# Two 256-column matmuls into one accumulator in place of one 512-column matmul and a fold

## The chip, the cores and the metric

The kernel runs on one core of one Trainium2 chip. The metric is the device time of one execution in microseconds (us); 2125.77 us is the median of 3 runs of the kernel before (2125.0 to 2126.07).

The core's engines run beside each other: PE (TensorE) does matmuls, and its weight loads are listed apart as PEld; DVE (VectorE) and ACT (ScalarE) do elementwise work and are the only two that read the matmuls' results out of PSUM here; POOL (GpSimd) does a little arithmetic; SP issues the DMAs. PSUM has eight banks, each of 512 fp32 columns on 128 partitions.

## The reference

A trunk of two residual layers on 256 tokens of width 2048: sparse attention with an MLP, then a gated short convolution with an MLP. Attention, norms and rotary embedding are left out here; what the change touches are the two kinds of product below, whose weights are read once each.

```python
def _short_conv_mixer(h, w_in, conv_w, w_out):
    b_gate, c_gate, u = jnp.split(h @ w_in, 3, axis=-1)       # w_in 2048 x 6144
    z = c_gate * u
    zp = jnp.pad(z, ((0, 0), (CONV_WIDTH - 1, 0), (0, 0)))
    y = sum(zp[:, j:j + S] * conv_w[j] for j in range(CONV_WIDTH))
    return (b_gate * y) @ w_out

def _sqrelu_mlp(h, w1, w2):
    a = jax.nn.relu(h @ w1)                                    # w1 2048 x 8192
    return (a * a) @ w2                                        # w2 8192 x 2048
...
for i in range(DEPTH):                                         # DEPTH = 2
    x = x + mixer(_rmsnorm(x, g))                              # 0: attention, 1: short conv
    x = x + _sqrelu_mlp(_rmsnorm(x, mlp_norm_g[i]), mlp_w1[i], mlp_w2[i])
```

## The kernel before

All large products are made in fp32 accuracy from float32r parts: each operand is the sum of a high part and a low part, and of the four products three are kept (high by high, high by low, low by high). The weights arrive by DMA as `raw` tiles; `split` (lines 202 and 203) makes from each the high part `wh` on ACT and the low part `wl` on DVE, four pieces ahead of PE. The tokens' operand tiles (`xp` from a norm, `hq` from a product) hold for one k-tile of 128 rows 256 columns of high parts and then 256 columns of low parts.

The work is a list of units. A unit is one accumulation over K into a set of PSUM banks, cut into pieces; the main loop at the end of the program takes one piece at a time: its matmuls (`matmuls`, line 210), at the unit's last piece the unit's `end`, one step of every generator of side work, and then the splits of pieces further on. The order on each engine is the order in which this loop emits instructions. There are two kinds of unit:

- Wide units (lines 229 to 231): the tokens' tile is the stationary operand, the weights stream past in 512 columns (384 and 336 in the first unit), three matmuls for each k-tile and bank.
- Tall units (lines 224 and 225): the weights are stationary, 128 output columns at a time, and the tokens stream past. They are used where the result is wanted with features on partitions: the first product of both MLPs (32 units) and the input product of the convolution (12 units). A tall unit makes 512 output columns in four blocks, each with a bank of its own (`W4`, line 849), from 16 k-tiles in 8 pieces of two. For a block and a k-tile, `wh` is matched with all 512 token columns, so that the bank's left half gathers high by high and its right half high by low; then `wl` is matched with the 256 high columns and adds into the left half. That is 44 x 4 x 16 = 2,816 pairs of matmuls.

At the end of a tall unit the halves of each bank are added: `fold` (line 760) copies the right half to SBUF on ACT (line 763) and adds the left half to it on DVE (line 764); `fold4` does so for the four banks. For an MLP, `h_gen` then squares the positive part (line 781, DVE) and `put_pair` (lines 756 and 757) splits the result into high and low for the next wide unit. In an MLP two tall units are followed by two wide ones that use their results; the first four k-tiles of the wide unit come from the first of the two tall ones, the next four from the second.

Of the kernel before, what the change touches and what calls it, by code (L numbers as in the profile page):

```python
# [18 lines left out]
P = 128  # L19
# [20 lines left out]

# 500000 ** -(j / 16), j = 0..15, then 500000 ** -(j / 8), j = 0..7, in float32
_F16 = [
# [11 lines left out]
class Unit:  # L54
    """One accumulation group over K, in ticks of kk k-tiles, on n columns of a weight.

    wide: out[token, column], banks of the given column widths for each of two token tiles.
    tall: out[column, (token by x high part, token by x low part)], a bank for 128 columns.
    """

# [8 lines left out]
def trunk(ctx: ExitStack, tc: tile.TileContext, x, positions, attn_norm_g, attn_w_in, attn_q_norm_g,  # L69
# [21 lines left out]

# [1 line left out]
    live = []  # L93
# [38 lines left out]

# [1 line left out]
    ident = sb.tile([P, P], F32, name="ident")  # L134
# [22 lines left out]

# [1 line left out]
    units = []  # L159
# [50 lines left out]
    def matmuls(p):  # L210
        u, i, _ = pieces[p]
        n, K = u.n, u.kk * u.ticks
        if i == 0:
            u.banks = [[bank() for _ in u.widths] for _ in range(1 if u.tall else 2)]
        hi, lo = piece_tiles.pop(p)
        for t, row in enumerate(u.banks):
            c = 0
            for o, w in zip(row, u.widths):
                for j in range(u.kk):
                    k = i * u.kk + j  # L220
                    wh, wl = (v[:, j * n + c : j * n + c + w] for v in (hi, lo))
                    xk = u.lhs(k)
                    if u.tall:
                        nc.tensor.matmul(o, wh, xk, start=(k == 0), stop=False)  # L224
                        nc.tensor.matmul(o[:, 0:256], wl, xk[:, 0:256], start=False, stop=(k == K - 1))  # L225
                    else:
                        ah = xk[:, t * P : (t + 1) * P]
                        al = xk[:, 256 + t * P : 256 + (t + 1) * P]
                        nc.tensor.matmul(o[:, :w], ah, wh, start=(k == 0), stop=False)  # L229
                        nc.tensor.matmul(o[:, :w], al, wh, start=False, stop=False)  # L230
                        nc.tensor.matmul(o[:, :w], ah, wl, start=False, stop=(k == K - 1))  # L231
                c += w

# [1 line left out]
    def rsqrt(v, n):  # L235
        """v**-0.5 for a [P, n] tile, by a bit guess and three Newton steps."""
        y, t = small(n), small(n)
        yi = y.bitcast(I32)
        nc.vector.tensor_scalar(yi, v.bitcast(I32), 1, None, op0=ALU.logical_shift_right)
        nc.vector.tensor_scalar(yi, yi, -1, 0x5F3759DF, op0=ALU.mult, op1=ALU.add)  # L240
        for _ in range(3):
            nc.gpsimd.tensor_tensor(t, y, y, ALU.mult)  # L242
            nc.gpsimd.tensor_tensor(t, t, v, ALU.mult)
            nc.gpsimd.tensor_scalar(t, t, -0.5, 1.5, op0=ALU.mult, op1=ALU.add)
            nc.gpsimd.tensor_tensor(y, y, t, ALU.mult)
        return y

# [1 line left out]
    def norm_gen(st, half):  # L249
        """Operand tiles of x*g for k-tiles of one half, and its part of the squares' sum."""  # L250
        if st["key"] != "attn":
# [61 lines left out]
    def norm_rows(key, power):  # L313
        """The token scale (or its square) of a norm along the free axis, [P, 256]."""
        st = norms[key]
        yield from wait((key, "rs"))
        yield from pause(3)
        rows = tmp()[:, 0:256]
        dg = tmp()
        for t in range(2):  # L320
            nc.vector.tensor_scalar(
                dg[:, t * P : (t + 1) * P], ident, st[power][:, t : t + 1], None, op0=ALU.mult
            )
        nc.vector.memset(dg[:, 256:384], 1.0)
        ps = yield from tp_get()
        yield
        for t in range(2):
            nc.tensor.matmul(
                ps[:, t * P : (t + 1) * P], dg[:, 256:384], dg[:, t * P : (t + 1) * P],
                start=True, stop=True,  # L330
            )
        yield
        nc.scalar.activation(rows, ps[:, 0:256], AF.Copy)
        tp_put()
        st[power + "rows"] = rows
        done.add((key, power + "rows"))
# [30 lines left out]

# [1 line left out]
    def add_to_x(nh, then=None, store=False, norm=None):  # L369
        def end(banks):  # L370
            for t in range(2):
                for b in range(2):
                    # the last bank of all leaves in two parts
                    w = 256 if store and nh and t and b else 512
                    for o in range(0, 512, w):
                        c = nh * 1024 + b * 512 + o
                        sl, ps = xs[t][:, c : c + w], banks[t][b][:, o : o + w]
                        if norm is None:
                            nc.vector.tensor_tensor(sl, ps, sl, ALU.add)
                        else:  # L380
                            rs_of(norm, t)
                            nc.vector.scalar_tensor_tensor(  # L382
                                sl, ps, norms[norm]["rs2"][:, t : t + 1], sl, op0=ALU.mult, op1=ALU.add
                            )
                        if store:
                            nc.sync.dma_start(out[0][t * P : (t + 1) * P, c : c + w], sl)
# [10 lines left out]

# [1 line left out]
    rope = sb.tile([P, 2, 4, RH + RI], F32, name="rope")  # L399
    NF = RH + RI  # L400

    def rope_tables():
        """rope[:, t, 0:4] = cos, cos, -sin, sin of position * frequency."""
        yield from pause(10)
# [24 lines left out]
    def rotate(v, t, heads, half, off):  # L429
        """Partial rotary on v [P, heads, dim] in place: its first 2*half dims."""  # L430
        c = rope[:, t, 0:2, off : off + half].unsqueeze(1).to_broadcast([P, heads, 2, half])
# [123 lines left out]
    def head_scale(sq, n, mul):  # L555
        """(mean of squares + eps)**-0.5 * mul from a list of squared [P, n*HD] tiles."""
        v = small(n * len(sq))
# [79 lines left out]
    def q_gen(n, qs, sqs):  # L637
# [16 lines left out]
        yield from wait("bias", "kT")  # L654
        # scores; a chunk is (token tile, heads, keys)
        chunks = [(0, (0, 1, 2, 3)), (1, (0, 1)), (1, (2, 3))]
# [77 lines left out]

# [1 line left out]
    Q = {}  # L736
# [12 lines left out]
    def put_pair(key, q, i, val):  # L749
        """Split [P, (2, 256)] fp32 into k-tiles 2i, 2i+1 of a quad."""  # L750
        if i == 0:
# [7 lines left out]

    def fold(dst, ps):  # L760
        """dst [P, 256] = the sum of a tall bank's two halves."""
        h = sbt([P, 256], "half", 4)
        nc.scalar.activation(h, ps[:, 256:512], AF.Copy)  # L763
        nc.vector.tensor_tensor(dst, ps[:, 0:256], h, ALU.add)  # L764

    def fold4(banks):
        r = [tmp(), tmp()]
        for c in range(4):
            fold(r[c // 2][:, c % 2 * 256 : (c % 2 + 1) * 256], banks[0][c])
        return r  # L770

# [1 line left out]
    def m1_end(key, q):  # L773
        def end(banks):
            live.append(h_gen(key, q, fold4(banks)))

        return end

    def h_gen(key, q, r):
        for i in range(2):  # L780
            nc.vector.scalar_tensor_tensor(r[i], r[i], 0.0, r[i], op0=ALU.max, op1=ALU.mult)  # L781
            put_pair(key, q, i, r[i])
            yield

# [1 line left out]
    C = {}  # L786

    def c_end(q):
        def end(banks):
            C["c", q] = fold4(banks)  # L790

        return end

    def u_end(q):
        def end(banks):
            live.append(y_gen(q, fold4(banks)))

        return end

    def b_end(q):  # L800
        def end(banks):
            live.append(by_gen(q, fold4(banks)))

# [42 lines left out]

# [1 line left out]
    W2 = [512, 512]  # L848
# [37 lines left out]

# [1 line left out]

# [16 lines left out]

    # transposes of no use but to have the tensor engine's clock up when x arrives
    ps = bank()
# [57 lines left out]
```

## Time and profile before

| | before |
|---|---|
| median of 3 runs | 2125.77 us |
| span of the profiled execution, first to last instruction | 2122.9 us |
| PE busy | 2112.0 us, 99% of the span |
| PEld busy | 1788.8 us, 84% |
| DVE busy | 1286.4 us, 61% |
| ACT busy | 977.2 us, 46% |
| POOL busy | 114.8 us, 5% |
| DMA | 392.66 MB, mean 185 GB/s |
| matmuls, weight loads | 10,714 and 10,714 |

The profiled execution is listed with its span alone; the medians are 2.9 us above it. Busy times of different engines overlap and don't add up to the span. A matmul is listed with a duration of its own that overlaps the next one's, since they are pipelined; what a matmul costs in a dense row of them is the distance from its start to the start of the next, called a step below.

### The profile page before, as it was taken

Reading aid. Unit: us, or ns where it says so; the run is one execution under the profiler, and the core shown is the slowest. Engines: PE = TensorE matmul, PEld = TensorE weight load, DVE = VectorE, ACT = ScalarE, POOL = GpSimd, SP = SyncE. Lnnn points to the kernel's source line nnn. Section 1 sums busy time; section 2 is a strip of 40 time slices with the busy share of each in tenths; the row PEclk is TensorE's granted clock in tenths of the full one; section 3 lists DMA queues with packets and bytes.
Section 4 is the critical chain, followed back from the end, with each engine's and each line's share of the span. In section 5 each row is a group of like instructions: output and inputs, shape, how many; then the busy total and the mean of one; then the engine's idle time right before and its main releaser. Section 6 shows DMA issues by size and latency. Waiting matters only on the chain.

```text
span 2122.9 us, 26675 instructions
## 1 busy us (share of the span) xinstructions
PE 2112.0 (99%) x10714; PEld 1788.8 (84%) x10714; DVE 1286.4 (61%) x1553; ACT 977.2 (46%) x1271; POOL 114.8 (5%) x220
## 2 busy tenths in 40 slices
PE   9999999999999999999999999999999999999999
PEld 8878778888888888888888888888888888888887
DVE  5587656655656556556666566556565565655654
ACT  5456545443444434444555454454444344443443
POOL 0333100000000000000011110001000000000000
PEclk9999999999999999999999999999999999999999
DMA  8544455556555565565555555556655566555653
GB/s 274 173 141 163 139 177 170 188 184 206 183 189 189 180 205 181 189 198 179 183 194 179 198 179 190 196 169 202 195 184 191 181 198 193 183 190 188 199 186 111
DMA packets 152268, 392.66 MB, mean 185 GB/s; under 512 B 6368, under 2 KB 7088, under 8 KB 152144
## 3 DMA queue, kind: packets, MB, share of 16 engines
q1 hardware_dynamic: 151888, 390.75, 56.6%
q8 instruction: 84, 1.38, 0.2%
q0 software_dynamic: 224, 0.19, 0.1%
q14 instruction: 40, 0.33, 0.0%
q10 hardware_dynamic: 32, 0.01, 0.0%
HBM read 388.83 MB, written 2.10 MB: 184 GB/s over the span
## 4 chain that ended last, share of the span: by engine, by line
PE 98%; POOL 1%; DMA 1%; DVE 0%; ACT 0%; issue 0%; SPq 0%; DVEq 0%; ACTq 0%
PE ps L224 30%; PE ps L230 16%; PE ps L231 16%; PE ps L229 16%; PE ps L225 16%; DMA raw<-in_attn_w_in 1%; PE ps L278 1%; PE ps L661 0%; PE ps L507 0%; PE ps L719 0%; PE ps L706 0%; POOL tmp L440 0%; POOL rot L436 0%; PE ps L646 0%; POOL tmp L439 0%; ACT wh L202 0%
## 5 line engine op out<-in xcount | busy, mean ns | idle before, releaser
L203 DVE TENSOR_TENSOR wl<-raw,wh 128x1024 fp32r<-128x1024 f32 (+2 forms) x738 | 890.1, 1225 | 551.7 <-ACT wh L202 551.1
L202 ACT ACTIVATE wh<-raw 128x1024 fp32r<-128x1024 f32 (+2 forms) x738 | 765.9, 1055 | 722.8 <-PE ps L230 390.2
L224 PE MATMUL ps<-xp,wh 128*128 128x512 f32 x2816 | 978.0, 392 | 0.0
L225 PE MATMUL ps<-xp,wl 128*128 128x256 f32 x2816 | 786.9, 279 | 0.0
L224 PEld LDWEIGHTS ps<-xp,wh 128*128 128x128 f32 x2816 | 529.8, 188 | 114.6
L225 PEld LDWEIGHTS ps<-xp,wl 128*128 128x128 f32 x2816 | 531.6, 189 | 0.8
L231 PE MATMUL ps<-wl,hq 128*128 128x512 f32 x1280 | 505.0, 395 | 0.0
L229 PE MATMUL ps<-wh,hq 128*128 128x512 f32 x1280 | 505.0, 395 | 0.0
L230 PE MATMUL ps<-wh,hq 128*128 128x512 f32 x1280 | 505.0, 395 | 0.0
L229 PEld LDWEIGHTS ps<-wh,hq 128*128 128x128 f32 x1280 | 240.9, 188 | 55.7 <-issue 0.5
L230 PEld LDWEIGHTS ps<-wh,hq 128*128 128x128 f32 x1280 | 240.3, 188 | 56.3 <-issue 0.5
L231 PEld LDWEIGHTS ps<-wl,hq 128*128 128x128 f32 x1280 | 240.7, 188 | 54.8
L764 DVE TENSOR_TENSOR tmp<-ps,half 128x256 f32<-128x256 f32 x176 | 74.7, 424 | 110.0 <-ACT half L763 110.0
L763 ACT ACTIVATE half<-ps 128x256 f32<-128x256 f32 x176 | 67.6, 384 | 152.3 <-PE ps L225 152.3
L382 DVE SCALAR_TENSOR_TENSOR x<-ps,rs_mlp,x 128x512 f32<-128x512 f32 x129 | 90.8, 746 | 53.0 <-PE ps L231 53.0
L229 PE MATMUL ps<-wh,xp 128*128 128x512 f32 (+2 forms) x288 | 114.2, 397 | 2.2 <-ACT wh L202 2.0
L230 PE MATMUL ps<-wh,xp 128*128 128x512 f32 (+2 forms) x288 | 108.0, 375 | 0.9 <-DVE xp L263 0.9
L231 PE MATMUL ps<-wl,xp 128*128 128x512 f32 (+2 forms) x288 | 108.1, 375 | 0.4 <-DVE wl L203 0.4
L756 ACT ACTIVATE hq<-tmp 128x512 fp32r<-128x512 f32 x72 | 45.5, 632 | 105.4 <-DVE tmp L781 93.0
L757 DVE TENSOR_TENSOR hq<-tmp,hq 128x512 fp32r<-128x512 f32 x72 | 51.1, 710 | 50.3 <-ACT hq L756 50.3
L242 POOL TENSOR_TENSOR small<-small 128x8 f32<-128x8 f32 (+1 forms) x27 | 14.0, 517 | 1011.3 <-DVE small L240 1009.7
L229 PEld LDWEIGHTS ps<-wh,xp 128*128 128x128 f32 x288 | 54.6, 190 | 12.5 <-ACT wh L202 2.4
(131 smaller groups left out, 661.9 us busy)
## 6 DMA issues: line engine op xcount, KB each, us to landing
raw<-in_mlp_w SPq DMA_DIRECT2D x256, 1024.0 KB, 5.4
raw<-in_conv_w_in SPq DMA_DIRECT2D x48, 1024.0 KB, 5.2
raw<-in_attn_w_in SPq DMA_DIRECT2D x24, 1024.0 KB, 5.3
raw<-in_attn_w_out SPq DMA_DIRECT2D x16, 1024.0 KB, 5.4
raw<-in_conv_w_out SPq DMA_DIRECT2D x16, 1024.0 KB, 5.4
raw<-in_attn_w_in SPq DMA_DIRECT2D x5, 1104.0 KB, 8.2
raw<-in_attn_w_in SPq DMA_DIRECT2D x5, 552.0 KB, 8.7
out_y<-x SPq DMA_DIRECT2D x7, 256.0 KB, 2.9
```

The lines of the kernel that those rows point to most:

```text
L202: nc.scalar.activation(hi[:, a], src[:, a], AF.Copy)
L203: nc.vector.tensor_tensor(lo[:, a], src[:, a], hi[:, a].bitcast(F32), ALU.subtract)
L224: nc.tensor.matmul(o, wh, xk, start=(k == 0), stop=False)
L225: nc.tensor.matmul(o[:, 0:256], wl, xk[:, 0:256], start=False, stop=(k == K - 1))
L229: nc.tensor.matmul(o[:, :w], ah, wh, start=(k == 0), stop=False)
L230: nc.tensor.matmul(o[:, :w], al, wh, start=False, stop=False)
L231: nc.tensor.matmul(o[:, :w], ah, wl, start=False, stop=(k == K - 1))
L382: nc.vector.scalar_tensor_tensor(sl, ps, norms[norm]["rs2"][:, t : t + 1], sl, op0=ALU.mult, op1=ALU.add)
L756: nc.scalar.activation(hi, val, AF.Copy)
L757: nc.vector.tensor_tensor(lo, val, hi.bitcast(F32), ALU.subtract)
L763: nc.scalar.activation(h, ps[:, 256:512], AF.Copy)
L764: nc.vector.tensor_tensor(dst, ps[:, 0:256], h, ALU.add)
```

## The change

In a tall unit the 512-column matmul is cut in two of 256 columns with the same `wh`: high columns and low columns of the tokens both add into the same 256 columns of PSUM, and `wl` adds there too. A block needs 256 columns, so two blocks share a bank, and a unit takes two banks where it took four. The bank's first matmul carries the start flag, for the left block alone. At the end there is nothing to fold: for the convolution `copied` moves each bank to SBUF on ACT; for the MLP ACT takes the positive part out of PSUM, and DVE multiplies it by the positive part read from PSUM. The wide units stand as they were (their three matmuls are only indented anew), and comments are gone from the file.

```diff
@@ matmuls
-            u.banks = [[bank() for _ in u.widths] for _ in range(1 if u.tall else 2)]
+            u.banks = [[bank() for _ in u.widths[::2]]] if u.tall else [[bank() for _ in u.widths] for _ in range(2)]
         hi, lo = piece_tiles.pop(p)
+        if u.tall:
+            for c in range(len(u.widths)):
+                o = u.banks[0][c // 2][:, c % 2 * 256 : c % 2 * 256 + 256]
+                for j in range(u.kk):
+                    k = i * u.kk + j
+                    wh, wl = (v[:, j * n + c * P : j * n + (c + 1) * P] for v in (hi, lo))
+                    xk = u.lhs(k)
+
+                    for w, x, first, last in (
+                        (wh, xk[:, 0:256], k == 0 and c % 2 == 0, False),
+                        (wh, xk[:, 256:512], False, False),
+                        (wl, xk[:, 0:256], False, k == K - 1),
+                    ):
+                        nc.tensor.matmul(o, w, x, start=first, stop=last, skip_group_check=True)
+            return
...
-                    if u.tall:
-                        nc.tensor.matmul(o, wh, xk, start=(k == 0), stop=False)
-                        nc.tensor.matmul(o[:, 0:256], wl, xk[:, 0:256], start=False, stop=(k == K - 1))
...
-    def fold(dst, ps):
-        """dst [P, 256] = the sum of a tall bank's two halves."""
-        h = sbt([P, 256], "half", 4)
-        nc.scalar.activation(h, ps[:, 256:512], AF.Copy)
-        nc.vector.tensor_tensor(dst, ps[:, 0:256], h, ALU.add)
-
-    def fold4(banks):
+    def copied(banks):
         r = [tmp(), tmp()]
-        for c in range(4):
-            fold(r[c // 2][:, c % 2 * 256 : (c % 2 + 1) * 256], banks[0][c])
+        for i in range(2):
+            nc.scalar.activation(r[i], banks[0][i], AF.Copy)
         return r
...
     def m1_end(key, q):
         def end(banks):
-            live.append(h_gen(key, q, fold4(banks)))
+            r = [tmp(), tmp()]
+            for i in range(2):
+                nc.scalar.activation(r[i], banks[0][i], AF.Relu)
+                nc.vector.scalar_tensor_tensor(r[i], banks[0][i], 0.0, r[i], op0=ALU.max, op1=ALU.mult)
+            live.append(h_gen(key, q, r))
...
     def h_gen(key, q, r):
         for i in range(2):
-            nc.vector.scalar_tensor_tensor(r[i], r[i], 0.0, r[i], op0=ALU.max, op1=ALU.mult)
             put_pair(key, q, i, r[i])
...
-            C["c", q] = fold4(banks)
+            C["c", q] = copied(banks)
...
-            live.append(y_gen(q, fold4(banks)))
+            live.append(y_gen(q, copied(banks)))
...
-            live.append(by_gen(q, fold4(banks)))
+            live.append(by_gen(q, copied(banks)))
```

PE, within a tall unit of the first MLP; `ps` is a bank, `xp` a k-tile of tokens, `wh` and `wl` the weights of one piece. First before, then now:

```order
L224 MATMUL ps_4547<-xp_3019,wh_4590 128x512
L225 MATMUL ps_4547<-xp_3019,wl_4591 128x256
L224 MATMUL ps_4547<-xp_3022,wh_4590 128x512
L225 MATMUL ps_4547<-xp_3022,wl_4591 128x256
L224 MATMUL ps_4548<-xp_3019,wh_4590 128x512
```

```order
L229 MATMUL ps_4808<-xp_3041,wh_4864 128x256 x2
L229 MATMUL ps_4808<-xp_3041,wl_4865 128x256
L229 MATMUL ps_4808<-xp_3044,wh_4864 128x256 x2
L229 MATMUL ps_4808<-xp_3044,wl_4865 128x256
L229 MATMUL ps_4808<-xp_3041,wh_4864 128x256 x2
```

Two matmuls for a block and a k-tile have become three, all of 256 columns, and the second block follows in the same bank. The built program has 13,530 matmuls and as many weight loads (10,714 of each in the profile of the kernel before): each matmul has a load of its own, the second one with the same `wh` too.

DVE, from the end of a tall unit of the first MLP to the next split; `half` and `tmp` are SBUF tiles. First before, then now:

```order
L764 TENSOR_TENSOR tmp_3849<-ps_3683,half_3851 128x256
L764 TENSOR_TENSOR tmp_3849<-ps_3684,half_3854 128x256
L764 TENSOR_TENSOR tmp_3850<-ps_3685,half_3857 128x256
L764 TENSOR_TENSOR tmp_3850<-ps_3686,half_3860 128x256
L781 SCALAR_TENSOR_TENSOR tmp_3849<-tmp_3849 128x512
L757 TENSOR_TENSOR hq_3864<-tmp_3849,hq_3864 128x2x256
L203 TENSOR_TENSOR wl_3868<-raw_3681,wh_3867 128x1024
```

```order
L783 SCALAR_TENSOR_TENSOR tmp_4015<-ps_3787,tmp_4015 128x512
L783 SCALAR_TENSOR_TENSOR tmp_4016<-ps_3788,tmp_4016 128x512
L768 TENSOR_TENSOR hq_4021<-tmp_4015,hq_4021 128x2x256
L203 TENSOR_TENSOR wl_4025<-raw_3785,wh_4024 128x1024
```

The four folds and the first of the two squares have become two operations that read PSUM; the split of the result (line 757, now 768) and that of the next weights follow as before.

## Rows read from the trace of the kernel before

**Rows 1.** Page, span and part 1: busy time and share of the engines.
```profile
span 2122.9 us, 26675 instructions
PE 2112.0 (99%) x10714; PEld 1788.8 (84%) x10714; DVE 1286.4 (61%) x1553; ACT 977.2 (46%) x1271; POOL 114.8 (5%) x220
```

**Rows 2.** Page, part 4: chain that ended last, shares of the span by engine.
```profile
PE 98%; POOL 1%; DMA 1%; DVE 0%; ACT 0%; issue 0%; SPq 0%; DVEq 0%; ACTq 0%
```

**Rows 3.** Waits of PE, the two longest in total, whole span: waiter, waited for, us, times, longest.
```profile
PE ps L229 <- ACT wh L202: 2.0, 1, 2.0
PE ps L909 <- POOL ident masks.py:199: 1.3, 1, 1.3
```

**Rows 4.** Groups of instructions by line: shapes, count, busy us, mean ns, idle before.
```profile
L224 PE MATMUL ps<-xp,wh 128*128 128x512 f32 x2816 | 978.0, 392 | 0.0
L225 PE MATMUL ps<-xp,wl 128*128 128x256 f32 x2816 | 786.9, 279 | 0.0
L225 PEld LDWEIGHTS ps<-xp,wl 128*128 128x128 f32 x2816 | 531.6, 189 | 0.8
```

**Rows 5.** Windows, two tall units, then two wide: length, busy us of engines, PEclk, DMA.
```profile
510.61:554.94 44.33, 44.33 (x257) 39.10 (x256) 25.32 (x29) 19.28 (x24) 0.00 (x0) 1.00 0.58 190
466.13:510.61 44.48, 44.48 (x194) 36.09 (x193) 27.22 (x29) 19.16 (x21) 0.00 (x0) 1.00 0.59 189
```

**Rows 6.** Timeline in a tall unit: start us, duration us, engine, line, operation.
```profile
984.14 0.28 PE L225 MATMUL ps<-xp,wl 128*128 128x256 f32 x1
984.14 0.19 PEld L224 LDWEIGHTS ps<-xp,wh 128*128 128x128 f32 x1
984.25 0.39 PE L224 MATMUL ps<-xp,wh 128*128 128x512 f32 x1
984.26 0.19 PEld L225 LDWEIGHTS ps<-xp,wl 128*128 128x128 f32 x1
```

**Rows 7.** Timeline, PE: the first and the last matmul of the 2,816 tall pairs.
```profile
331.09 0.39 PE L224 MATMUL ps<-xp,wh 128*128 128x512 f32 x1
...
2072.78 0.28 PE L225 MATMUL ps<-xp,wl 128*128 128x256 f32 x1
```

**Rows 8.** Timeline, PE, first unit: six steps of 384 columns, then three of 336.
```profile
41.91 0.34 PE L229 MATMUL ps<-wh,xp 128*128 128x384 f32 x1
...
42.96 0.32 PE L229 MATMUL ps<-wh,xp 128*128 128x336 f32 x1
...
43.42 0.33 PE L229 MATMUL ps<-wh,xp 128*128 128x384 f32 x1
```

**Rows 9.** Windows inside tall units: DVE and ACT little busy, then much; columns as in rows 5.
```profile
437.27:442.26 4.99, 4.99 (x30) 4.40 (x29) 2.01 (x2) 1.20 (x2) 0.00 (x0) 1.00 0.55 185
1100.36:1105.31 4.95, 4.95 (x31) 4.38 (x29) 4.88 (x8) 3.76 (x5) 0.00 (x0) 1.00 0.71 225
```

**Rows 10.** Groups by line: folds, square, and the nearest operations that read a bank.
```profile
L382 DVE SCALAR_TENSOR_TENSOR x<-ps,rs_mlp,x 128x512 f32<-128x512 f32 x129 | 90.8, 746 | 53.0 <-PE ps L231 53.0
L764 DVE TENSOR_TENSOR tmp<-ps,half 128x256 f32<-128x256 f32 x176 | 74.7, 424 | 110.0 <-ACT half L763 110.0
L763 ACT ACTIVATE half<-ps 128x256 f32<-128x256 f32 x176 | 67.6, 384 | 152.3 <-PE ps L225 152.3
L781 DVE SCALAR_TENSOR_TENSOR tmp<-tmp 128x512 f32<-128x512 f32 x64 | 43.7, 683 | 0.0
L711 ACT ACTIVATE tmp<-ps 128x512 f32<-128x512 f32 x12 | 6.3, 599 | 5.1 <-PE ps L706 5.1
```

**Rows 11.** Timeline after a tall unit: its consumer's first matmul, and its first operand tiles.
```profile
466.13 0.39 PE L229 MATMUL ps<-wh,hq 128*128 128x512 f32 x1
...
468.47 0.69 DVE L757 TENSOR_TENSOR hq<-tmp,hq 128x512 fp32r<-128x512 f32 x1 [0.70 <-ACT hq L756]
```

**Rows 12.** Timeline: the longest dense row of short matmuls with a load each (transposes).
```profile
175.39 1.47 PE L706 MATMUL ps<-ident,tmp 128*128 128x128 f32 x12
```

More of the change, by code (lines that the diff above doesn't have):

```diff
@@ L222, in matmuls @@
                     xk = u.lhs(k)
-                    if u.tall:
-                        nc.tensor.matmul(o, wh, xk, start=(k == 0), stop=False)
-                        nc.tensor.matmul(o[:, 0:256], wl, xk[:, 0:256], start=False, stop=(k == K - 1))
[L226 to L231, printed above, removed]
+                    ah = xk[:, t * P : (t + 1) * P]
+                    al = xk[:, 256 + t * P : 256 + (t + 1) * P]
+                    nc.tensor.matmul(o[:, :w], ah, wh, start=(k == 0), stop=False)
+                    nc.tensor.matmul(o[:, :w], al, wh, start=False, stop=False)
+                    nc.tensor.matmul(o[:, :w], ah, wl, start=False, stop=(k == K - 1))
                 c += w
```

## The prediction

> **What bounds the kernel now.** I read the page's busy shares first, then the chain of work that ended last, then the waits of PE. PE is busy 99% of the 2122.9 us span, DVE 61%, ACT 46% [rows 1]. A busy PE could still be a waiting one, so the chain decides: 98% of the span is PE [rows 2], and the two largest items in the list of what PE waited for are 2.0 and 1.3 us, once each [rows 3]. No other engine and no DMA holds PE up. So only a change in PE's own steps can move the time, by 0.2% (4.25 us, about what a measurement of this kernel can tell from no change) or more.
>
> The step is the distance between the starts of two matmuls; the listed durations, 392 and 279 ns [rows 4], overlap. In a tall unit a 256-column matmul starts at 984.14 and the next pair's 512-column one at 984.25 [rows 6]. Over all 2,816 pairs, from the first start to the last [rows 7], the step after a 512-column matmul is 230.1 ns on average and the step after a 256-column one 116.7 ns: 346.8 ns for a pair. The windows agree: 128 pairs in 44.33 us are 346.3 ns [rows 5]. The wide units have 192 matmuls of 512 columns in 44.48 us, 231.7 ns each [rows 5]. All this is at a granted clock of 1.00, so the clock has nothing to give.
>
> **What the change takes away, off the path.** 176 folds: 67.6 us on ACT and 74.7 us on DVE; and 64 squares, 43.7 us on DVE [rows 10]. What comes instead is bounded by the nearest reads of a full bank: 88 operations on ACT by 599 ns are 52.7 us, and 64 on DVE by 746 ns are 47.7 us [rows 10]. ACT falls by some 15 us and DVE by some 71 us. I cost both at nothing, since neither engine stands in the chain: the work that covers them is PE's own row of matmuls. The place where a unit's result is due shows how good that cover is. After the tall units the wide unit starts at 466.13, and the first operand tile from the later tall unit is complete at 468.47 + 0.69 = 469.16 [rows 11]; it is first used after four pieces of 12 steps of 231.7 ns, at 477.2. There were 8 us to spare, and the new end is shorter. New waits are DVE's for ACT's positive part (one for each bank, where it waited for the copied halves before), with the next weight splits queued behind; those run four pieces ahead, and PE hardly ever waited for one [rows 3]. Two banks for a unit instead of four lengthen the time until a bank comes round again. Transfers, weight splits and the wide units stay.
>
> **What it adds, on the path.** For each block and k-tile, 512 + 256 columns become three times 256: 768 columns before and after. What is new is one more matmul and one more weight load, 2,816 of each, and the question is what a step of 256 columns costs when others of its kind follow it.
>
> The nearest row is the 256-column matmul itself: 116.7 ns, already with a weight load beside it, because the load for the next matmul starts together with the 256-column matmul (both at 984.14) and the next matmul starts 0.11 us later [rows 6]. By it a triple takes 3 x 116.7 = 350.1 ns, 3.3 ns more than the pair; 2,816 x 3.3 ns = **9.3 us**. Put differently, half of the 512-column step is 115.0 ns, and each matmul pays about 1.7 ns beyond its columns.
>
> The bounds on both sides: below, 115.0 ns for 256 columns, which also comes out if the pair's 346.8 is taken with the wide units' 231.7 for the 512 columns (115.1). Then the triple takes 345.0 ns, 1.8 ns less, and the change is worth -5.1 us. Above, the first unit's narrower steps: six of 384 columns take 1.05 us, 175.0 ns each, and three of 336 take 0.46 us, 153.3 ns each [rows 8]. A line through 336 columns at 153.3 and 512 at 231.7 gives 117.7 ns at 256, a triple of 353.1 ns, and +17.7 us. I take 116.7, because it is measured on these very operands and lies between the two.
>
> On the fixed price of a matmul the Trainium skill (TensorE: Matmul & The Clock Gate, Back-to-back issue gap) has a rule that speaks against the change: a warm step is the columns divided by 2.4 GHz plus about 2.5 ns, whatever their number. By the page 512 columns would take 215.8 ns and 256 would take 109.2; the trace has 230.1 and 116.7, so the columns are dearer here than the page has them, and the measurement decides. By the page's 2.5 ns alone the sum would be +7.0 us (an estimate from that page) where the rows give +9.3.
>
> **The sum.** Span 2122.9 + 9.3 = 2132.2 us; the median stands 2.9 us above the span, so 2135.1 us, 0.44% slower.
>
> **Rivals.**
> (a) Columns alone count. PE's time follows the number of columns streamed, which doesn't change; the extra matmul and load disappear in the pipeline. For it: the pair's 346.8 ns for 768 columns is no more, by column, than the wide units' 231.7 for 512 (347.6 for 768), though it has more matmuls in it. Against it: the separate steps of 512 and 256, and the narrow ones of 336 and 384, all cost more by column the shorter they are [rows 5, 8]. Time: between -5.1 and 0, so 2120.7 to 2125.8, mostly within 0.2%.
> (b) Faster: relief of DVE and ACT reaches PE. A 512-column step takes 230.1 ns where one column in each cycle of 2.4 GHz would take 213.3; if that excess came from the other engines' traffic to PSUM and SBUF, less traffic would speed PE up. The excess is 26.8 ns a pair, 75 us over the tall units; ACT and DVE lose 86 of 2264 us, 3.8% [rows 1]; with the excess of the wide units (3,840 steps by 18.4 ns, 71 us), 3.8% of 146 us is 5.5 us: 2120 us. It decides if PE's pace follows the other engines' load. The windows speak against it: 29 steps take 4.99 us with DVE busy 2.01 and ACT 1.20, and 4.95 us with 4.88 and 3.76 [rows 9].
> (c) Much slower: the weight load becomes the step. Before, every second load had a 230 ns step to hide in; now all have 117, and a load is listed with 189 ns [rows 4]. If a load had to end before its matmul starts, a triple would take 567 ns: 2,816 x 220 ns = 620 us, 2746 us. Rows 6 excludes that for a single short step, since the next matmul starts long before its load's 0.19 us are over. A milder debt, which builds up when short steps follow each other, is bounded by twelve transposes with a load each in 1.47 us, at most 122.5 ns a step [rows 12]: a triple of 367.5, +58 us, 2184 us. The same page of the Trainium skill (The mechanism, on what overlaps and what doesn't) states that a load overlaps matmuls in flight only for other rows of the array, which would be the harsher case; the trace disagrees, with 0.11 us between the starts in rows 6.
> (d) The change doesn't do what it says: the weights aren't kept, since every matmul of the built program has its own load. That is in the forecast. Were the chip to skip the second load, nothing would be won, as the load lies beside the stream already.
>
> **How the numbers follow.** The forecast, a fixed price for one more matmul, has 0.64; its small end, a step under 116.3 ns, falls within 0.2%, which I give 0.04 of it. Rival (a) has 0.24, 0.04 of it faster by more than 0.2% and 0.20 within. Rival (b) has 0.04, (c) 0.08; (d) is no separate time. So slower 0.60 + 0.08 = 0.68, within 0.2% 0.24, faster 0.08. The range reaches from inside rival (a) to above the upper bound of 17.7 us, with room for a few ns of (c): 2122 to 2146.
>
> **What the changed kernel's profile would show.** Right: 8,448 matmuls of 256 columns with steps of 116 to 118 ns, two tall units in about 44.8 us where 44.33 stood, wide units unchanged at 231.7 ns a step, 13,530 loads, DVE's busy time near 1216 us and ACT's near 962, and PE's waits as small as before. A step of 115 ns means (a). A drop in the wide units' steps too means (b). Steps above 120 ns, with each start behind the end of a load, mean (c). Wrong in another way: if PE begins to wait at the end of tall units, for a bank or for `hq`, then my cover of 8 us was not there; and if the time of first and second `wh` step differ, the second load matters after all.

## The result, and the profile after

The changed kernel takes 2145.1 us (median of 4 runs, 2143.66 to 2146.46) against 2125.62 us before: a ratio of 1.0093, 95% interval 1.0079 to 1.0107, that is 19.5 us slower, where 9.3 had been forecast. The profiled execution has a span of 2143.8 us, 20.9 more than before; the median stands 1.3 us above it, where the prediction's sum has 2.9. Ratios and intervals, here and below, leave out one execution among all, of the kernel whose `wl` matmul reads the low columns, that took 7496.58 us.

The page of the changed kernel, busy times and the chain by engine:

```profile
PE 2133.0 (99%) x13530; PEld 1925.0 (90%) x13530; DVE 1214.7 (57%) x1377; ACT 962.1 (45%) x1183; POOL 111.9 (5%) x220
...
PE 99%; DMA 1%; SPq 0%; DVE 0%; ACT 0%; issue 0%; DVEq 0%
```

PE is 99% of the chain, as good as all of it, as in [rows 2], and there are 2,816 more matmuls and loads. DVE went down by 71.7 us and ACT by 15.1 against [rows 1]. What PE waited for, the two largest items of that list:

```profile
PE ps L240 <- ACT xp L273: 2.3, 1, 2.3
PE ps L240 <- ACT wh L202: 2.0, 1, 2.0
```

They stand beside those of [rows 3]: no wait at the ends of the tall units, for a bank or for `hq`. The first lies at the program's start, 18.6 us into the span, and was 0.2 us in the kernel before. The MLP ends' own operations are these, by line (count, busy us, mean ns, idle before):

```profile
L783 DVE SCALAR_TENSOR_TENSOR tmp<-ps,tmp 128x512 f32<-128x512 f32 x64 | 44.3, 692 | 108.7 <-ACT tmp L782 108.7
L782 ACT ACTIVATE tmp<-ps 128x512 f32<-128x512 f32 x64 | 38.3, 598 | 131.8 <-PE ps L229 131.8
```

The windows show where the time went. Columns as in [rows 5]: the stretch, its length, busy us of PE, PEld, DVE, ACT and POOL with counts, granted clock, DMA share and rate. First two tall units, then two wide ones, of the changed kernel:

```profile
514.25:559.53 45.28, 45.28 (x385) 45.27 (x384) 23.36 (x23) 18.37 (x20) 0.00 (x0) 1.00 0.57 186
...
469.76:514.25 44.49, 44.49 (x194) 36.07 (x193) 25.96 (x27) 19.37 (x21) 0.00 (x0) 1.00 0.59 189
```

The wide units take what they took in [rows 5], 44.49 against 44.48 us. The tall ones take 45.28 against 44.33: 128 triples of 353.8 ns in place of 128 pairs of 346.3. Over the 14 such stretches of each kernel that hold nothing else the means are 353.6 and 346.4 ns; 2,816 x 7.2 ns = 20.3 us, against 20.9 us between the spans and 19.5 between the medians. The timeline of PE within a tall unit (start us, duration us; two matmuls of the same form are merged in one row):

```profile
627.97 0.28 PE L229 MATMUL ps<-xp,wl 128*128 128x256 f32 x1
628.09 0.40 PE L229 MATMUL ps<-xp,wh 128*128 128x256 f32 x2
628.33 0.28 PE L229 MATMUL ps<-xp,wl 128*128 128x256 f32 x1
```

From the start of the first `wh` matmul to that of `wl` it is 0.24 us. On average over all triples those two steps take 237.0 ns together, 118.5 each, and the step after `wl` takes 116.9. So the one 512-column step of 230.1 ns has become 237.0, and the rest is as it was. (The view gives starts to 0.01 us, so these averages can be off by 0.2 ns.)

### The profile page after: what moved, and what is told of

Its sections match the earlier page's. It is cut to its first block, busy times and chain, and to the rows that moved or that the text cites. A ratio compares the mean times of both kernels' runs of the same rounds, so it can differ in the third digit from the quotient of the medians.

```text
span 2143.8 us, 32060 instructions
## 1 busy us (share of the span) xinstructions
PE 2133.0 (99%) x13530; PEld 1925.0 (90%) x13530; DVE 1214.7 (57%) x1377; ACT 962.1 (45%) x1183; POOL 111.9 (5%) x220
## 4 chain that ended last, share of the span: by engine, by line
PE 99%; DMA 1%; SPq 0%; DVE 0%; ACT 0%; issue 0%; DVEq 0%
PE ps L229 46%; PE ps L241 17%; PE ps L242 17%; PE ps L240 17%; PE ps L289 1%; DMA raw<-in_attn_w_in 1%; PE ps L672 0%; PE ps L518 0%; PE ps L730 0%; PE ps L717 0%; PE ps L657 0%; SPq L899 0%; DVE x L393 0%; PE ps L499 0%; DVE wl L203 0%; SPq L182 0%
## 5 line engine op out<-in xcount | busy, mean ns | idle before, releaser
L229 PE MATMUL ps<-xp,wh 128*128 128x256 f32 x5632 | 998.2, 281 | 0.0
L229 PEld LDWEIGHTS ps<-xp,wh 128*128 128x128 f32 x5632 | 860.7, 188 | 1.5
L783 DVE SCALAR_TENSOR_TENSOR tmp<-ps,tmp 128x512 f32<-128x512 f32 x64 | 44.3, 692 | 108.7 <-ACT tmp L782 108.7
L782 ACT ACTIVATE tmp<-ps 128x512 f32<-128x512 f32 x64 | 38.3, 598 | 131.8 <-PE ps L229 131.8
L240 PEld LDWEIGHTS ps<-wh,xp 128*128 128x128 f32 x288 | 55.3, 192 | 14.6 <-ACT xp L273 2.5
L241 PEld LDWEIGHTS ps<-wh,xp 128*128 128x128 f32 x288 | 55.1, 191 | 11.0 <-issue 2.4
L242 PEld LDWEIGHTS ps<-wl,xp 128*128 128x128 f32 x288 | 55.0, 191 | 8.9 <-DVE wl L203 0.4
```

Of the source, the lines that this page charges most:

```text
L229: nc.tensor.matmul(o, w, x, start=first, stop=last, skip_group_check=True)
L782: nc.scalar.activation(r[i], banks[0][i], AF.Relu)
L783: nc.vector.scalar_tensor_tensor(r[i], banks[0][i], 0.0, r[i], op0=ALU.max, op1=ALU.mult)
```

## The experiments

Two questions were open: which part of the edit costs 7.2 ns a triple, and what sets a step of 256 columns, the stream (its columns passing through, with a fixed price) or the load of the next weights. All times are compared with runs of the kernel before on the same chip.

**The cut alone.**

```diff
-                        nc.tensor.matmul(o, wh, xk, start=(k == 0), stop=False)
+                        nc.tensor.matmul(o[:, 0:256], wh, xk[:, 0:256], start=(k == 0), stop=False, skip_group_check=True)
+                        nc.tensor.matmul(o[:, 256:512], wh, xk[:, 256:512], start=False, stop=False, skip_group_check=True)
-                        nc.tensor.matmul(o[:, 0:256], wl, xk[:, 0:256], start=False, stop=(k == K - 1))
+                        nc.tensor.matmul(o[:, 0:256], wl, xk[:, 0:256], start=False, stop=(k == K - 1), skip_group_check=True)
```

> The kernel before, with one edit: the 512-column matmul of a tall pair is cut in two of 256 columns that write the left and the right half of the bank as before; folds and banks stay. Theory F (each further matmul pays a fixed price, about 6.9 ns, wherever it writes): a triple takes 353 to 354 ns as in the changed kernel, +20 us against before. Rival S (the price comes from adding into the same 256 PSUM columns three times running): the two wh matmuls now write different columns, so the triple falls back to 346 to 349 ns, 0 to +6 us. The forecast's own step of 116.7 ns would be 350.1, +9 us.

Measured: 2144.66 us, ratio 1.0093 (1.0078 to 1.0108), as slow as the changed kernel. The timeline of PE, and the window of two tall units:

```profile
628.32 0.28 PE L224 MATMUL ps<-xp,wh 128*128 128x256 f32 x1
628.44 0.28 PE L225 MATMUL ps<-xp,wh 128*128 128x256 f32 x1
628.56 0.28 PE L226 MATMUL ps<-xp,wl 128*128 128x256 f32 x1
628.67 0.28 PE L224 MATMUL ps<-xp,wh 128*128 128x256 f32 x1
```

```profile
514.84:560.11 45.27, 45.27 (x385) 45.27 (x384) 25.31 (x29) 19.37 (x24) 0.00 (x0) 1.00 0.58 187
```

Here each matmul has its own row: the steps average 118.9, 118.0 and 117.1 ns, and the window is 45.27 us where the changed kernel has 45.28. With folds, four banks and separate columns the price is the same. So adding into the same columns, sharing a bank and the new ends cost nothing that these runs can tell; the cut into two matmuls is all of it.

**The folds' worth.** The add of a fold is left out, and ACT copies the left half alone:

```diff
-        h = sbt([P, 256], "half", 4)
-        nc.scalar.activation(h, ps[:, 256:512], AF.Copy)
-        nc.vector.tensor_tensor(dst, ps[:, 0:256], h, ALU.add)
+        nc.scalar.activation(dst, ps[:, 0:256], AF.Copy)
```

> The kernel before with its pairs of matmuls as they are; the folds' adds on DVE are left out, and ACT copies the left half of a bank alone, so the product of the high weights with the low tokens is missing from the result. All theories in which ACT and DVE are off the path: pair 346.8 ns, 0 us within 0.2%. Rival (relief of DVE and ACT reaches PE): 75 us less DVE work, up to -5 us.

Measured: 2125.28 us, ratio 0.9999 (0.999 to 1.0008). The page's busy times, beside [rows 1]:

```profile
PE 2112.1 (99%) x10714; PEld 1788.7 (84%) x10714; DVE 1216.8 (57%) x1377; ACT 976.9 (46%) x1271; POOL 113.4 (5%) x220
```

DVE has 70 us less and PE's time is 2112.1 as before. What the change saves on DVE is worth nothing here, within some 0.1% of the time.

**Stream or load.** First an uneven cut, 384 and 128 columns, with the kernel before otherwise as it was:

> The kernel before, with the 512-column matmul of a tall pair cut in 384 and 128 columns. Theory F (fixed price, 6.9 ns and 0.436 ns a column): steps of 174 and 63 ns and the 116.9 of wl, a triple of 354 ns, +20 us as with the cut at 256. Rival L (the weight load sets the least step, between the transposes' 108 ns and the 118.5 seen in the changed kernel): the 128-column step can't fall below 108 to 118 ns, a triple of 399 to 410 ns, +148 to +177 us.

Measured: 2287.83 us, ratio 1.0765 (1.0749 to 1.0781): 162.5 us slower, within what the load as a floor gives. The timeline, PE and then the loads:

```profile
627.94 0.34 PE L224 MATMUL ps<-xp,wh 128*128 128x384 f32 x1
628.12 0.22 PE L225 MATMUL ps<-xp,wh 128*128 128x128 f32 x1
628.17 0.33 PE L226 MATMUL ps<-xp,wl 128*128 128x256 f32 x1
628.35 0.34 PE L224 MATMUL ps<-xp,wh 128*128 128x384 f32 x1
```

```profile
628.12 0.19 PEld L226 LDWEIGHTS ps<-xp,wl 128*128 128x128 f32 x1
628.23 0.19 PEld L224 LDWEIGHTS ps<-xp,wh 128*128 128x128 f32 x1
```

This has to be read with care. The 128-column step is 59.2 ns on average, no floor at all; but the matmul behind it is listed with 0.33 us where a 256-column one has 0.28, and its step is 170.1 instead of 117. My reading is that it is put down as started while its weights are still coming. The load for the matmul after that starts 0.11 us behind the previous load and not with the matmul. The two steps are 229.3 ns together, two loads of 114.65. So a floor by the load explains both steps, and it lies close below 117.

How close, and on which side a 256-column step stands, two sizes on either side tell. Three matmuls of n columns (192 or 288) replace the pair from the second k-tile on:

```diff
-                        nc.tensor.matmul(o, wh, xk, start=(k == 0), stop=False)
-                        nc.tensor.matmul(o[:, 0:256], wl, xk[:, 0:256], start=False, stop=(k == K - 1))
+                        for ww, m in ((wh, n), (wh, n), (wl, n)) if k else ((wh, 512), (wl, 256)):
+                            nc.tensor.matmul(
+                                o[:, 0:m], ww, xk[:, 0:m], start=(k == 0 and m == 512), stop=(k == K - 1 and ww is wl)
+                            )
```

> The kernel before with its tall pairs (from the second k-tile of a unit on, 2,640 of 2,816) replaced by three matmuls of 192 columns each, wh, wh, wl, all on the first 192 token columns; the rest of the tokens is left out there. The step at 256 columns can be set by the stream or by the load of the next weights, which the cut at 384 showed to take 114.65 ns when loads follow each other. Theory F alone (6.9 ns and 0.436 ns a column): steps of 90.6, a triple of 272 ns, 2640 x -75 = -198 us against before. Theory F with a load floor of 114.65: a triple of 344 ns, -7 us. Theory L (the load alone sets the 118.5): a triple of 354 ns, +19 us.

> As the kernel with 192 columns, but with three matmuls of 288 columns on the first 288 token columns (the result differs from the reference's there). Theory F: steps of 132.4, a triple of 397 ns, 2640 x 50.5 = +133 us against before; with a price by columns alone (0.4528) 391 ns, +117 us. With a floor that still binds there the triple would be longer than 397.

Measured: 2094.07 us with 192 columns, ratio 0.9851 (0.9832 to 0.9871), and 2256.74 us with 288, ratio 1.0617 (1.0595 to 1.0638), two runs each. Windows of two tall units, 192 and then 288 columns:

```profile
507.31:550.28 42.97, 42.97 (x377) 42.62 (x376) 25.29 (x29) 19.25 (x24) 0.00 (x0) 1.00 0.61 195
```

```profile
524.10:574.49 50.39, 50.39 (x378) 50.05 (x377) 25.50 (x29) 19.37 (x24) 0.00 (x0) 1.00 0.53 168
```

Each window holds 8 pairs (370 ns each in the first kernel, 349 in the second, by their starts) and 120 triples. That leaves 333.4 ns for a triple of 192 columns and 396.7 for one of 288, steps of 111.1 and 132.2 ns. By its columns a step of 192 would be 90.6: it stands on the floor, which is 111 ns when load follows load. The 512-column step behind such triples, 253 ns on average where it has 230 in the kernel before, shows the wait of a late load in the same place as above. At 288 it is the 132.4 that the fixed price and the columns give. A 256-column step, 116.9 to 118.9 ns, stands above the floor: the stream sets it. Theory F with a floor agrees with all three sizes, and the load's length as the cause of the 118.5 falls. Whether the fixed part of a step belongs to the matmul or to the change of weights between two matmuls, no run separates, since every matmul here has a load of its own. The time with 192 columns went down by 31 us and not 7, since the floor is 111 and not 114.65.

PEld is as good as always busy in both windows, and in the changed kernel's too (45.27 of 45.28 us), though only the first is held up by loads. Loads are listed with 188 ns each and overlap; a full PEld shows no bound here.

**The same cut in the wide units.** Every 512-column matmul there is cut in two of 256, the tall units stay:

> The kernel before with every 512-column matmul of the wide units (4,416) cut in two of 256 columns; the tall units stay. Theory F (every further matmul pays): two steps of 118.5 in place of one of 231.8 to 230.1, 5 to 7 ns each, +23 to +30 us. Rival T (the price belongs to the tall operands, weights stationary and tokens moving): 0 us.

Measured: 2140.41 us, ratio 1.0072 (1.0057 to 1.0087): 15.1 us for 4,416 cuts, 3.4 ns each on average, between the two expectations. The window of two wide units:

```profile
470.73:516.02 45.29, 45.29 (x386) 45.29 (x385) 27.32 (x29) 19.19 (x21) 0.00 (x0) 1.00 0.56 186
```

It is 45.29 us where 44.48 stood [rows 5], 4.2 ns a cut. Its 384 steps are 117.9 ns each, the same as in the tall units; but the 512-column step that they replace was 231.7 there [rows 5] and 230.1 in the tall pair. So the step of 256 columns is common to both kinds, and the price of a cut differs because the uncut step does.

**The small differences between steps.** Five kernels looked for what makes the step after `wl` 1.6 ns shorter than those after `wh`, and the tall 512-column step shorter than the wide one.

> The changed kernel with the order wh by high, wl by high, wh by low in each triple, so that no load repeats the weights before it. Theory F: the triple stays at 353 to 354 ns and the time within 2 us of the changed kernel's 2145. Rival R (loading the same weights twice running costs extra): the triple falls to about 350 ns, some 10 us less than the changed kernel. Also seen: whether the step after wl stays at 116.9 and those after wh at 118.5 when their places are swapped.

Measured: 2147.52 us, ratio 1.0104 (1.0087 to 1.0121); the triple is 354.9 ns, a little above what was expected and no shorter: a repeated load of the same weights costs nothing extra that shows. The step after `wl` is 117.4 in the middle place too.

> The changed kernel with other values in the low parts of the weights: DVE writes the larger of raw and high part instead of their difference, so that the products with wl are wrong but read the same tiles at the same places. If the shorter step after wl (116.9 against 118.5 ns) comes from the values (low parts), it rises to 118.5 and the time by 2816 x 1.6 = 4.5 us over the changed kernel. If it comes from place or addresses, nothing changes (2145 us).

Measured: 2143.98 us, ratio 1.0089 (1.0072 to 1.0106); the step after `wl` is 117.1. These values make no difference.

> The changed kernel with wh in place of wl in the third matmul of each triple (a third product of the high weights; the product with the low weights is left out). In the changed kernel the two steps after wh take 118.5 ns each and the one after wl 116.9. If the shorter step belongs to the operand wl, all three steps take 118.5: a triple of 355.5, +1.5 ns, 4 us over the changed kernel's 2145. If it belongs to the third place or to the change of k-tile behind it, the triple stays at 353.9, 0 us.

Measured: 2137.85 us, ratio 1.0057 (1.0042 to 1.0072). The triple is 351.8 ns, shorter and not longer; and the wide units, whose code is untouched, were shorter as well, some by 1 ns a step. Neither expectation covers the time.

> The changed kernel with wl in place of wh in the second matmul (the product of the high weights with the low tokens is left out, another stands in its place). If the shorter step belongs to the operand wl: 118.5 + 2 x 116.9, a triple of 352.3, 4 to 5 us under the changed kernel's 2145. If what counts is that the weights change between two matmuls or stay the same tile, wh-wl-wl has as many changes as wh-wh-wl: 0 us.

Measured: 2142.72 us, ratio 1.0079 (1.0062 to 1.0096). The triple is 353.0 ns, half of what was expected of `wl`; and the short step, 116.7, is now the one after the single `wh`, with 118 to 119 after the two `wl`. So it doesn't belong to `wl`; all orders together lie between 351.8 and 354.9 ns a triple.

> The kernel before, where the wl matmul of a tall pair reads the low token columns instead of the high ones (another product, so the result differs). In the tall pairs the 512-column step is 230.1 ns and in the wide units 231 to 233, and in both the shorter steps are those whose next matmul streams from the same start as this one. Theory K (streaming from the same start again saves some 2 ns): the 512-column step rises to about 232, a pair of 348.5, +4 to +5 us. Otherwise (the place of the streamed columns doesn't count): 0 us.

Measured: 2125.45 us, ratio 1.0003 (0.9993 to 1.0012); pairs of 346.4 ns. Theory K falls.

The pieces show what the averages hide: the steps repeat every five pieces, and `wh` and `wl` lie in rings of five buffers (`AHEAD + 1`, in `split`), while `raw`, `xp` and `hq` have rings of 4, 16 and 4. Three pieces of a tall unit of the kernel with `wh` three times, 24 steps of 256 columns each (a piece, the next, and the fifth after that):

```profile
516.03:518.91 2.88, 2.88 (x26) 2.88 (x25) 1.57 (x2) 1.06 (x1) 0.00 (x0) 1.00 0.85 255
518.91:521.63 2.72, 2.72 (x26) 2.72 (x25) 1.22 (x1) 1.06 (x1) 0.00 (x0) 1.00 0.93 291
...
532.97:535.69 2.72, 2.72 (x26) 2.72 (x25) 0.53 (x1) 0.60 (x1) 0.00 (x0) 1.00 0.57 227
```

These are steps of 120 ns, then 113, then 113 again. Two pieces of the kernel before, eight pairs each:

```profile
521.66:524.46 2.80, 2.80 (x18) 2.46 (x17) 1.22 (x1) 1.06 (x1) 0.00 (x0) 1.00 0.66 178
...
530.01:532.75 2.74, 2.74 (x19) 2.42 (x18) 0.92 (x3) 1.16 (x3) 0.00 (x0) 1.00 0.48 188
```

That is 350 and 342 ns a pair; the step after `wl` alone runs from 114.5 to 119.0 ns there, by buffer, and 116.7 is its average over the five. The kernel without the folds' adds has the same pattern, so those adds have no part in it. The small differences go with the buffer at least as much as with the operand's name. What it is about a buffer stays open: no run changed the ring.

**An order that might beat the kernel before.** With the wide units' loop turned so that both token tiles stream the same weights one after the other:

```diff
...
+                    for v, part, last in ((wh, 0, False), (wh, 256, False), (wl, 0, k == K - 1)):
+                        for t in range(2):
+                            nc.tensor.matmul(
+                                u.banks[t][b][:, :w], xk[:, part + t * P : part + (t + 1) * P], v,
+                                start=(k == 0 and v is wh and part == 0), stop=last,
+                            )
...
```

> The kernel before with the wide units' matmuls in another order: for a bank's columns and k-tile both token tiles by their high and low parts stream the same wh one after the other, then both stream wl; two changes of the streamed operand in six matmuls where there were four. Tall units stay. Theory K: 3.8 ns less for six matmuls, 784 times, -3 us, 2122. Otherwise (231.8 ns a step whatever the order): 0 us. A rival that makes it slower: banks alternate with each matmul, and if that costs what the step after wl shows (1 ns), +5 us.

Measured: 2127.01 us, ratio 1.0012 (1.0003 to 1.0021), by 1.7 us slower if anything. No version here that does the whole work beats the kernel before (the one with 192 columns leaves part of it out).

## Why the prediction was right in its sign and wrong in its size

The bound was read rightly: PE's steps are the time, and nothing else moved it. The cover for the folds and for the new ends held, since PE has no wait at the ends and a kernel without the folds' adds is as fast as the kernel before. DVE's 1214.7 and ACT's 962.1 us are what the sum off the path gave (1216 and 962). The sign was right, and for the reason given: one more matmul for the same columns.

The step that failed is the price of the 256-column step, in "What it adds, on the path". I had 115.0 and 117.7 as bounds and took 116.7, "because it is measured on these very operands". That was the step after `wl`, and I gave it to the two `wh` matmuls too. They measured 118.5 each on average in the changed kernel, above my upper bound; the step after `wl` measured 116.9 as foreseen. The term was 3.3 ns a triple and is 7.2: 20.3 us where 9.3 stood. The time lies inside the range all the same, 0.9 us from its upper end; that end stood there for the bound of 17.7 us and for rival (c), so the forecast can take no credit from it.

The rows left room for this. The price of a cut is twice the 256-column step less the 512-column step that it replaces. Steps of 336 columns (153.3) [rows 8] and the tall pair's own 512 (230.1) lie on a line of 0.436 ns a column and 6.7 ns fixed, which gives 118.4 at 256 columns, 6.7 ns a cut and 19 us in all. But that line takes its two ends from different operands, and it is picked with the result in hand; through the wide units' 231.7, as I drew it, it gives 117.7, and 15 us when only the two `wh` steps have it. What could be known is that 116.7 was an average of steps from 114.5 to 119.0 ns, by buffer, in an alternation with long ones: a spread larger than the 3.3 ns a triple that I worked out from it. Why two of the three steps come out longer on average stays open.

Two more workings were off, neither of them in the sum. "About 1.7 ns beyond its columns" takes half of the 512-column step for columns alone, though that step has a fixed price too; the two steps, 230.1 and 116.7, give 3.3 ns a matmul. And rival (b) counts 3,840 steps of 512 columns in the wide units where there are 4,416. The sign named last, different steps after the first and the second `wh`, did appear (118.9 and 118.0 in the cut alone), but the order without repeated loads was no faster, so it doesn't show that the second load matters.

Of the rivals, (a), columns alone, fell: with the same columns written to the same places as before, the cut alone costs 19.3 us more. (b), relief by DVE and ACT, fell with the kernel without folds. (c), the load as the step, was not the cause, but it was nearer than I put it: the floor is 111 ns, and 7 ns lie between it and a step of 256 columns. (d): every matmul does have a load of its own, the second with the same `wh` too; as foreseen it is hidden, and the order without repeated loads is no faster.

On the Trainium skill (TensorE: Matmul & The Clock Gate, Back-to-back issue gap): its fixed price of about 2.5 ns a matmul gave +7.0 us as an estimate from that page. The sign agrees; the runs here show 7.2 ns for a cut in the tall units and 3.4 to 4.2 in the wide ones.

## What to carry to other kernels

Where PE is the chain, as here, work saved on other engines was worth nothing, and a matmul of full width cut in two was paid for, though the columns are the same: 3 to 7 ns for each cut, which 2,816 of them made into 0.9%. Before a step is carried over to a row that the trace doesn't show, look how far it varies from piece to piece: here 114.5 to 119.0 ns by buffer, more than the price that was to be worked out from it. A single step lifted out of an alternating pattern gave the price its sign here, not its size. And look how near the short steps come to the floor that the weight loads set (111 ns here, where 118 was the step), since a few columns fewer buy nothing beyond it.

## What the runs showed of the hardware that was not expected

- Behind a 128-column matmul the next one starts 59 ns later, is listed 0.05 us longer than usual, and the step after it is 170 instead of 117 ns. I read this as a listed start that lies before the weights have come.
- With a load for each matmul a row of 192-column matmuls steps at 111 ns, and the 128-column transposes of [rows 12] at 108 to 110, although a load is listed with 188 to 191 ns; PEld is listed as busy 99% or more at 192, 256 and 288 columns alike.
- The steps of float32r matmuls at a granted clock of 1.00 were, on average, 117 to 119, 132, 153, 174 to 176 and 230 to 233 ns for 256, 288, 336, 384 and 512 columns.
- A step of 256 columns goes with the buffers that hold the weights: 113 to 120 ns in one kernel, repeating every five pieces. The order and the choice of operands move the average triple by up to 3 ns (351.8 to 354.9). Why one buffer is slower than another was not found.
